# Row maxima of a differential attention branch: 96 rows for each map, or 32 rows with the two maps of a head in two row groups of TensorE

## The chip, the cores and the metric

The kernel runs on one core of one Trainium2 chip. The metric is the device time of one execution in microseconds (us). Lower is better. All times of before are in this document's section on the profile.

## The reference, cut to what matters

The kernel is one layer: a normalized input goes through one input projection, three attention branches (latent attention, differential attention, attention to 256 memory tokens), a gate and an output projection. The differential branch has 4 heads of two softmax maps each, over 2048 tokens, causal:

```python
def diff_branch(dq, dk, dv, pos, qn_g, kn_g, lam_vecs, subln_g, lam_init):
    ...
    q = rope(q, pos).reshape(b, s, DIFF_HEADS, 2, DIFF_D)
    k = rope(k, pos).reshape(b, s, DIFF_HEADS, 2, DIFF_D)
    ...
        sc = jnp.einsum('bqhmd,bkhmd->bhmqk', qblk, k).astype(jnp.float32) * scale
        sc = jnp.where(causal_mask(start, s)[None, None, None], sc, NEG_INF)
        p = jax.nn.softmax(sc, axis=-1)
        a = (p[:, :, 0] - lam * p[:, :, 1]).astype(v.dtype)
    ...
```

`DIFF_D` is 32. The softmax needs a row maximum, or a number near it, before its exponentials. The kernel gets that number in a pass of its own.

## The kernel before, in words

**Numbers as pairs.** Queries, keys, values and weights are kept as two fp16 parts, a high one and a low one. A product of two such numbers is three products: high by high, low by high, high by low. In the differential branch the three stand above each other in one contraction: for each map a column of `kT` (keys) and of `qB` (queries) holds 128 rows, which are 32 rows high, 32 low or high, 32 high or low, and 32 of which the first carries the row maximum (L441 to L461). A matmul over rows 0 to 96 then gives the score with its maximum taken off.

**The row-maximum pass** is `est_block` (L374 to L407). It is called for a step (a group `g` of two heads and a block `b` of 512 queries) and a head `i`, with `nmap` 2 for the differential branch (L464 to L472) and 1 for the latent one. Before, it goes over the maps `m`, then over the four tiles `t` of 128 queries, then over the key blocks `c` up to `b`. For each it multiplies 128 queries by up to 512 keys on rows 0 to 95 (L384), adds the mask on the diagonal with an identity of 128 rows (L386), and reduces the result: for block 0 with a maximum on VectorE (L388), for the others with a copy to bf16 on ScalarE (L390, L393), a maximum of two tiles on VectorE (L394) and a fold at the end of every second `t` (L397 to L399). The tile `er` of that fold has one buffer. The products lie in three PSUM buffers (`pe`). When a head is done, its stack with the maximum is transposed into `qB` (L470), and only then may the scores of that head start.

**What sets the order.** The code is one loop that advances generators (preparation of steps, fills such as projections, heads and tails of softmax maps) by planned positions. Priorities follow from that, and a scheduler then puts the instructions of each engine in an order, so one generator's matmuls stand between those of others. From 200 us to 747 us TensorE does the row-maximum pass and the scores and values of the differential branch (L384, L386, L546, L549, L502 to L505) with projections (L176 to L178) between them. From 747 us to 1340 us the latent branch follows (L812 to L894, its own L384), and to the end the output projection (L930 to L932).

**Other places the change touches.** The memory tokens' keys `mk1` and `mk2` lie in the pool of constants (L200, L201); they are the operands of L632, L653 and L654. The pool `kvp` has five buffers under the tag `kT`, in turn for weights at the start, the memory branch's queries `qA` and the keys `kT` of the differential branch.

Of the kernel before, what the change touches and what calls it, by code (L numbers as in the profile page):

```python
# [19 lines left out]
P = 128  # L20
# [20 lines left out]
def hybrid_block(ctx: ExitStack, tc: tile.TileContext, x, mem, positions, norm_g, w_in, mla_q_norm_g,  # L41
# [21 lines left out]

# [1 line left out]
    ident = cst.tile([P, P], BF16, name="ident")  # L65
# [37 lines left out]

# [1 line left out]
    def stage(name, pool=None):  # L105
# [10 lines left out]
    def load(dst, src, pace=PACE):  # L116
        """At the start, loads take turns with the transposes on the DMA queues."""
        if 0 < len(turned) < 2 * NPACE:
            with tc.issue_after(turned[max(0, len(turned) - pace)].ins):
                SP.dma_start(dst, src)  # L120
        else:
            SP.dma_start(dst, src)
# [18 lines left out]

# [1 line left out]
    def load_w(w, cols, gains, name, out, pool=None, ahead=2, pace=PACE):  # L143
        """Column ranges of w as fp16 pairs: NK views [P, 2, n] appended to out."""
        n = sum(c for _, c in cols)
        kpu = 2 if n > 256 else 4

        def fetch(i):
            st = stage(f"wst_{name}{i}", pool).rearrange("p (k c) -> p k c", k=2)
            at = 0  # L150
            for c0, c in cols:
                load(st[:, :, at:at + c], w[0, 2 * i * P:(2 * i + 2) * P, c0:c0 + c].rearrange("(k p) c -> p k c", p=P), pace)
                at += c
            return st

        sts = [fetch(i) for i in range(ahead - 1)]
        yield 1.0
        for i in range(NK // 2):
            if i + ahead - 1 < NK // 2:
                sts.append(fetch(i + ahead - 1))  # L160
                yield 1.0
            st = sts[i]
            if 2 * i % kpu == 0:
                wt = bigt([P, kpu, 2, 1024 // kpu], f"w_{name}{i}")
            for k in range(2):
                g = gains[:, 2 * i + k:2 * i + k + 1]
                dst = wt[:, (2 * i + k) % kpu]
                A.activation(dst[:, 0, :n], st[:, k, :n], AF.Copy, scale=g)
                V.scalar_tensor_tensor(dst[:, 1, :n], st[:, k, :n], g, dst[:, 0, :n], ALU.mult, ALU.subtract)
                out.append(dst)  # L170
            yield 1.0
# [8 lines left out]
    def project_block(hts, units, n, dst):  # L180
        """dst: [P, 4, >= n]"""
        for t in range(4):
# [10 lines left out]

# [1 line left out]
    top = tc.cur_priority  # L195
# [3 lines left out]
    V.tensor_tensor(g_mk, g_mk, g_mq, ALU.mult)  # L199
    mk1 = cst.tile([P, 2, 4, P], F16, name="mk1")  # L200
    mk2 = cst.tile([P, 2, 4, P], F16, name="mk2")  # L201
    mv = cst.tile([P, 2, 4, 130], F16, name="mv")
# [3 lines left out]
    def mem_kv():  # L206
# [30 lines left out]
        G.memset(s2[:, :, 64:128], MS)  # L237
        SP.dma_start_transpose(mk1.rearrange("p t h k -> p (t h) k"), s1.rearrange("p a b c -> p (a b c)"))
        SP.dma_start_transpose(mk2.rearrange("p t h k -> p (t h) k"), s2.rearrange("p a c -> p (a c)"))
        vv = kv[:, 0:2, 256:512].rearrange("p t (h d) -> p t h d", d=64)  # L240
# [5 lines left out]

# [1 line left out]
    cos_t = cst.tile([P, NT, 16], F32, name="cos_t")  # L248
# [63 lines left out]
    def rope_tabs(b, g, name):  # L312
        """cos and sin of block b's tokens with the halves of the gain folded in."""
        tb = wk.tile([P, 2, 4, 32], F32, tag="rtab", name=f"rt_{name}", bufs=1)
# [9 lines left out]
    def rope(dst, src, tb, nh, eng, name):  # L324
        """dst, src: [P, 4, nh, 32]"""
        tmp = tmp4(f"rtmp_{name}")[:, 0:128 * nh].rearrange("p (t h d) -> p t h d", t=4, d=32)
# [8 lines left out]
    def rope_in_place(q, tb, nh, eng, tmp):  # L335
        """q: [P, 4, nh, 32]"""
        tmp = tmp.rearrange("p (t h d) -> p t h d", t=4, d=32)
# [7 lines left out]

# [1 line left out]
    zsc = dr.tile([3, P, NT, 2 * P], F32, name="zsc")  # L347
# [5 lines left out]
    def put_v(vt, ps):  # L353
        """vt: [P, 2, 130], ps: [P, 2, 64] in PSUM, WS times the values"""
        A.activation(vt[:, :, 0:64], ps, AF.Copy, scale=1.0 / WS)
        V.scalar_tensor_tensor(vt[:, :, 65:129], ps, 1.0 / WS, vt[:, :, 0:64], ALU.mult, ALU.subtract)

    def put_gate(z, ps):
        """2 WS silu of the products ps"""
        A.activation(z, ps, AF.Tanh, scale=0.5 / WS)  # L360
# [10 lines left out]

# [1 line left out]
    def est_block(st, i, nmap, mcol, lhs, rhs):  # L373
        b = st.b  # L374
        mx = sm.tile([P, nmap, 4, 2], F32, tag="mx", name=f"mx{i}_{st.name}", bufs=2)
        fold = b >= EB
        for m in range(nmap):
            for t in range(4):
                if fold and t % 2 == 0:
                    er = wk.tile([P, 2, 512], BF16, tag="er", name="er", bufs=1)  # L380
                for c in range(b + 1):
                    ps = ps_e.tile([P, 512], F32, tag="pe", name="pe")
                    n = (4 if c < b else t + 1) * P
                    T.matmul(ps[:, 0:n], lhsT=lhs(m, t), rhs=rhs(m, c, n // P), start=True, stop=c < b)  # L384
                    if c == b:
# [3 lines left out]
                    elif c == 0:  # L389
                        A.activation(er[:, t % 2], ps, AF.Copy)  # L390
                    else:
                        ec = wk.tile([P, 512], BF16, tag="ec", name="ec", bufs=3)
                        A.activation(ec[:, 0:n], ps[:, 0:n], AF.Copy)  # L393
                        V.tensor_tensor(er[:, t % 2, 0:n], er[:, t % 2, 0:n], ec[:, 0:n], ALU.max)  # L394
                    yield 0.5
                if fold and t % 2:
                    for n in (256, 128, 64):  # L397
# [10 lines left out]

# [1 line left out]
    def prep_d(st, units):  # L410
# [29 lines left out]
        for w in (1, 0):  # L440
# [4 lines left out]
            for i in range(2):  # L445
                dst = stack([P, 4, 2, 4, 32], f"s{w}{i}_{nm}")
                src = r4[:, :, 2 * i:2 * i + 2, :]
                G.memset(dst[:, :, :, 3, :], MS if w else 0.0)
                at_hi, at_lo = ((0, 2), 1) if w else ((0, 1), 2)
                for k in at_hi:  # L450
                    A.activation(dst[:, :, :, k, :], src, AF.Copy)
                V.tensor_tensor(dst[:, :, :, at_lo, :], src, dst[:, :, :, 0, :], ALU.subtract)
                if w:
# [12 lines left out]
        for i in range(2):  # L466
            q4 = st.qs[i].rearrange("p t m r d -> p t m (r d)")
            yield from est_block(st, i, 2, lambda m: q4[:, :, m, 96], lambda m, t: st.qB[i][0:96, t, m, :],
                                 lambda m, c, n: st.kTs[c][0:96, i, 0:n, m, :])
            SP.dma_start_transpose(st.qB[i].rearrange("p t m k -> p (t m) k"), st.qs[i].rearrange("p t m r d -> p (t m r d)"))  # L470
# [3 lines left out]
    class Map:  # L474
        """One softmax map of one block of queries."""

# [39 lines left out]
    def finish(st, y, ct, ys, keep=False):  # L516
        """y: [P, 4, 128], already gated; its fp16 parts go out transposed."""
        b = st.b
# [63 lines left out]

# [1 line left out]
    def prep_m(st, units):  # L584
# [36 lines left out]
    def est_m(st):  # L621
# [6 lines left out]
        for i in range(2):  # L628
            for t in range(4):
                ps = ps_e.tile([P, 512], F32, tag="pe", name="pe")  # L630
                for k in range(2):
                    T.matmul(ps[:, 256 * k:256 * k + 256], lhsT=st.qA[:, i, t, k, :], rhs=mk1[:, :, 2 * i + k, :],  # L632
                             start=(k == 0), stop=(k == 1), skip_group_check=True)
# [8 lines left out]
    def maps_m(st):  # L642
# [7 lines left out]
        for h in range(4):  # L650

            def scores(ps, j, t0, n, diag, h=h):
                T.matmul(ps, lhsT=mk1[:, j, h, :], rhs=st.qA[:, h // 2, :, h % 2, :], start=True, stop=False)  # L653
                T.matmul(ps, lhsT=mk2[:, j, h, :], rhs=st.qB[h // 2][:, :, h % 2, :], start=False, stop=True)  # L654

# [15 lines left out]

# [1 line left out]
    def gates(b, chunk, units):  # L673
        """2 WS silu(z) of two groups for one block, kept in DRAM."""
        for t in range(4):
# [7 lines left out]

# [1 line left out]
    krot, ss_kr = [], []  # L685
# [68 lines left out]

# [1 line left out]
    wuq, wukv = [], []  # L756
# [146 lines left out]

# [1 line left out]
    wout = {}  # L905
# [17 lines left out]
    def out_tile(yt, t, hf, acc):  # L923
        """Adds the product of the given channel tiles to one [128, 512] tile of acc."""
        ps = ps_p.tile([P, 512], F32, tag="pp", name="pp")
# [9 lines left out]
    def out_dm():  # L935
        """x plus the products of the differential and memory channels, kept in DRAM."""
        yield from load_wout(range(4, 8))
# [31 lines left out]
    def out_last():  # L969
        """All but the last channel tile for the last block, kept on chip."""  # L970
        b = NB - 1
# [31 lines left out]

# [1 line left out]
    zcol = 1440  # L1005
# [230 lines left out]
```

## Time and profile before

| what | value |
|---|---|
| median of 3 runs | 1418.45 us |
| lowest and highest run | 1413.12 us, 1423.48 us |
| span of the profiled execution, first to last instruction | 1420.8 us |
| matmuls on TensorE in it | 13552, busy 92% of the span |
| granted TensorE clock, mean | 0.982 of full speed |

The profiled execution has no time of its own beside its span: 1420.8 us lies between the runs, 2.4 us above their median. In the profile, PE is TensorE's matmuls and PEld its weight loads, DVE is VectorE, ACT ScalarE, POOL GpSimd and SP SyncE, which issues the DMAs. A duration of a matmul runs to the modelled end of its pipeline; the next one starts earlier, so the pace is read from the starts.

### The profile page before, as it was taken

The numbers are of one execution on the slowest core, as the hardware profiler recorded it, in microseconds if no ns is written. First come the engines' busy times: TensorE is split into PE (matmuls) and PEld (weight loads), VectorE is DVE, ScalarE is ACT, GpSimd is POOL, SyncE is SP. The second block draws the span as 40 slices with busy tenths as digits, with TensorE's granted clock in tenths as the row PEclk, the third lists the DMA queues.
The fourth block names the chain that finished last, engine by engine and source line by source line (L and its number), as shares of the span: only waits on it lengthen the run. The fifth ranks groups of instructions, "written<-read, shape, count | busy, mean of one in ns | idle before, by whom it ended". The sixth has DMA issues, their size and how long they took to land. (4 is left out here: it accounts for less than half of the span.)

```text
span 1420.8 us, 35214 instructions
## 1 busy us (share of the span) xinstructions
PE 1312.4 (92%) x13552; PEld 831.7 (59%) x13552; DVE 1120.2 (79%) x2649; ACT 897.6 (63%) x2153; POOL 359.8 (25%) x541
## 2 busy tenths in 40 slices
PE   4789899999999999998998999999999899989998
PEld 1344456667676666677775665655655565555554
DVE  3458787889789958888899788977788999975645
ACT  5646444677777747786776676655776788664521
POOL 2222133303052044122321233533124433200000
PEclk9899999999999999999999999999999999999999
DMA  8999754223223223347245156255544454264352
GB/s 211 244 211 196 162 111 100 53 66 69 52 53 76 39 35 64 68 123 196 97 98 134 50 153 167 57 127 125 110 87 87 105 94 75 54 142 153 113 204 78
DMA packets 302696, 157.67 MB, mean 111 GB/s; under 512 B 248384, under 2 KB 281280, under 8 KB 302528
## 3 DMA queue, kind: packets, MB, share of 16 engines
q1 hardware_dynamic: 302496, 155.42, 47.6%
q8 instruction: 106, 1.74, 0.5%
q14 instruction: 62, 0.51, 0.1%
q0 software_dynamic: 32, 0.00, 0.0%
HBM read 61.79 MB, written 34.34 MB: 68 GB/s over the span
## 5 line engine op out<-in xcount | busy, mean ns | idle before, releaser
L492 ACT ACTIVATE p<-st 128x512 f32<-128x512 f32 (+3 forms) x672 | 354.6, 547 | 177.6 <-PE st L892 60.5
L493 DVE TENSOR_TENSOR plo<-p 128x512 f16<-128x512 f32 (+3 forms) x672 | 407.5, 617 | 60.1 <-ACT p L492 56.0
L505 PEld LDWEIGHTS <-plo 128*128 128x128 f16 x2304 | 217.5, 99 | 52.1 <-DVE plo L493 31.8
L502 PEld LDWEIGHTS <-p 128*128 128x128 bf16 x2304 | 219.1, 98 | 49.0 <-issue 2.3
L504 PEld LDWEIGHTS <-p 128*128 128x128 bf16 x2304 | 218.2, 98 | 29.4 <-issue 0.6
L393 ACT ACTIVATE ec<-pe 128x512 bf16<-128x512 f32 (+3 forms) x384 | 196.3, 537 | 40.5 <-PE pe L386 18.8
L394 DVE TENSOR_TENSOR er<-er,ec 128x512 bf16<-128x512 bf16 (+3 forms) x384 | 143.6, 380 | 33.5 <-ACT ec L393 20.4
L502 PE MATMUL pv<-V_d,p 128*128 128x65 f16 x1088 | 140.8, 193 | 0.8 <-DVE y_d L557 0.8
L504 PE MATMUL pv<-V_d,p 128*128 128x64 f16 x1088 | 140.7, 195 | 0.0
L502 PE MATMUL pv<-V_a,p 128*128 128x65 f16 x1088 | 139.4, 194 | 0.2
L504 PE MATMUL pv<-V_a,p 128*128 128x64 f16 x1088 | 139.2, 195 | 0.0
L505 PE MATMUL pv<-V_d,plo 128*128 128x65 f16 x1088 | 134.8, 192 | 4.5 <-DVE plo L493 3.9
L505 PE MATMUL pv<-V_a,plo 128*128 128x65 f16 x1088 | 130.6, 193 | 8.5 <-DVE plo L493 7.9
L390 ACT ACTIVATE er<-pe 128x512 bf16<-128x512 f32 x192 | 109.6, 604 | 38.3 <-DVE mx_d L399 14.2
L176 PEld LDWEIGHTS <-ht_x 128*128 128x128 f16 x896 | 88.5, 99 | 70.9 <-DMA ht_x<-xh_x 20.2
L890 PE MATMUL st<-qB_a,kT_a 97*128 97x512 f16 (+1 forms) x320 | 112.1, 350 | 18.0 <-ACT p L492 17.2
L177 PEld LDWEIGHTS <-ht_x 128*128 128x128 f16 x896 | 88.4, 99 | 55.5 <-issue 9.3
L178 PEld LDWEIGHTS <-ht_x 128*128 128x128 f16 x896 | 88.4, 99 | 54.5 <-DMA ht_x<-xl_x 4.6
L546 PE MATMUL st<-qB_d,kT_d 97*128 97x512 f16 (+1 forms) x320 | 109.2, 349 | 9.1 <-ACT p L492 8.3
L384 PE MATMUL pe<-kT_d,qB_d 96*128 96x512 f16 (+2 forms) x320 | 106.0, 350 | 8.2 <-ACT ec L393 4.7
L891 PE MATMUL st<-qB_a,kT_a 96*128 96x512 f16 (+1 forms) x320 | 112.0, 350 | 0.0
L892 PE MATMUL st<-qB_a,kT_a 96*128 96x512 f16 (+1 forms) x320 | 111.4, 348 | 0.0
(285 smaller groups left out, 3383.9 us busy)
## 6 DMA issues: line engine op xcount, KB each, us to landing
xt_x<-in_x_dram SPq DMA_DIRECT2D x16, 512.0 KB, 4.6
xr<-in_x_dram SPq DMA_DIRECT2D x16, 512.0 KB, 3.6
part<-xr SPq DMA_DIRECT2D x16, 512.0 KB, 3.0
ysc<-yt SPq DMA_DIRECT2D x31, 256.0 KB, 2.2
yl<-ysc SPq DMA_DIRECT2D x15, 512.0 KB, 4.3
zsc<-zc SPq DMA_DIRECT2D x48, 128.0 KB, 2.3
xa<-part SPq DMA_DIRECT2D x12, 512.0 KB, 3.6
out_dram<-xa SPq DMA_DIRECT2D x12, 512.0 KB, 2.7
```

What stands on the lines that cost most here:

```text
L390: A.activation(er[:, t % 2], ps, AF.Copy)
L393: A.activation(ec[:, 0:n], ps[:, 0:n], AF.Copy)
L394: V.tensor_tensor(er[:, t % 2, 0:n], er[:, t % 2, 0:n], ec[:, 0:n], ALU.max)
L492: A.activation(p32[:, :n], ps[:, :n], AF.Exp, scale=self.scale)
L493: V.tensor_tensor(plo[:, :n], p32[:, :n], phi[:, :n], ALU.subtract)
L502: T.matmul(pvv[:, t, 0:65], lhsT=phi[:, c], rhs=vt[:, 0:65], start=(j == 0 and t == 0), stop=False, skip_group_check=True)
L504: T.matmul(pvv[:, t, 0:64], lhsT=phi[:, c], rhs=vt[:, 65:129], start=False, stop=False, skip_group_check=True)
L505: last["pv"] = T.matmul(pvv[:, t, 0:65], lhsT=plo[:, c], rhs=vt[:, 0:65], start=False, stop=(j == self.njt - 1), skip_group_check=True)
L546: T.matmul(ps[:, :n], lhsT=st.kTs[j // 4][0:97, h, j % 4, m % 2, :], rhs=st.qB[h][0:97, t0:4, m % 2, :], start=True, stop=not diag)
L890: T.matmul(ps[:, :n], lhsT=kt[0:97, h, j % 4, 0, :], rhs=q[0:97, 0, t0:4, :], start=True, stop=False)
L891: T.matmul(ps[:, :n], lhsT=kt[0:96, h, j % 4, 0, :], rhs=q[0:96, 1, t0:4, :], start=False, stop=False)
L892: T.matmul(ps[:, :n], lhsT=kt[0:96, h, j % 4, 1, :], rhs=q[0:96, 0, t0:4, :], start=False, stop=not diag)
```

## The change

The pass goes over `t`, then `c`, and inside that over both maps. The matmul of map `m` reads rows 32m to 32m + 31 only, which hold the high parts of both operands (so the row maximum comes from the high parts alone). For this the second map's stack has its parts in another order: rows 32 to 63 of its keys and queries are now high parts. The mask still takes an identity of 128 rows. `er` gets two buffers, for both branches. To make room, `mk1` and `mk2` become one tile in the pool `kvp` under the tag `kT`.

```diff
-    mk1 = cst.tile([P, 2, 4, P], F16, name="mk1")
-    mk2 = cst.tile([P, 2, 4, P], F16, name="mk2")
+    mk = []
...
+        mk12 = kvp.tile([P, 2, 2, 4, P], F16, tag="kT", name="mk12")
+        mk.extend([mk12[:, 0], mk12[:, 1]])
...
     def est_block(st, i, nmap, mcol, lhs, rhs):
...
-        for m in range(nmap):
-            for t in range(4):
-                if fold and t % 2 == 0:
-                    er = wk.tile([P, 2, 512], BF16, tag="er", name="er", bufs=1)
-                for c in range(b + 1):
-                    ps = ps_e.tile([P, 512], F32, tag="pe", name="pe")
-                    n = (4 if c < b else t + 1) * P
-                    T.matmul(ps[:, 0:n], lhsT=lhs(m, t), rhs=rhs(m, c, n // P), start=True, stop=c < b)
+        ers = {}
+        for t in range(4):
+            if fold and t % 2 == 0:
+                for m in range(nmap):
+                    ers[m] = wk.tile([P, 2, 512], BF16, tag="er", name=f"er{m}", bufs=2)
+            for c in range(b + 1):
+                n = (4 if c < b else t + 1) * P
+                pss = [ps_e.tile([P, 512], F32, tag="pe", name="pe") for m in range(nmap)]
+                for m in range(nmap):
+                    T.matmul(pss[m][:, 0:n], lhsT=lhs(m, t), rhs=rhs(m, c, n // P), start=True, stop=c < b)
+                for m in range(nmap):
+                    ps = pss[m]
                     if c == b:
                         T.matmul(ps[:, t * P:n], lhsT=ident, rhs=mask_e, start=False, stop=True)
...
-                at_hi, at_lo = ((0, 2), 1) if w else ((0, 1), 2)
+                rows = dst.rearrange("p t m r d -> p t (m r) d")
+                at_hi, at_lo = ((slice(0, 5, 4), slice(2, 6, 3)), slice(1, 7, 5)) if w else \
+                    ((slice(0, 6, 5), slice(1, 7, 5)), slice(2, 5, 2))
                 for k in at_hi:
-                    A.activation(dst[:, :, :, k, :], src, AF.Copy)
-                V.tensor_tensor(dst[:, :, :, at_lo, :], src, dst[:, :, :, 0, :], ALU.subtract)
+                    A.activation(rows[:, :, k, :], src, AF.Copy)
+                V.tensor_tensor(rows[:, :, at_lo, :], src, rows[:, :, at_hi[0], :], ALU.subtract)
...
-            yield from est_block(st, i, 2, lambda m: q4[:, :, m, 96], lambda m, t: st.qB[i][0:96, t, m, :],
-                                 lambda m, c, n: st.kTs[c][0:96, i, 0:n, m, :])
+            yield from est_block(st, i, 2, lambda m: q4[:, :, m, 96], lambda m, t: st.qB[i][32 * m:32 * m + 32, t, m, :],
+                                 lambda m, c, n: st.kTs[c][32 * m:32 * m + 32, i, 0:n, m, :])
```

The order of the instructions moves with it. In the kernel after, the matmul of the pass is L387 and its mask L391. On TensorE, at the start of the pass for block 3 of the first group, head 0 (`qB0_d03`), before; `pe` with its number is the PSUM tile of one product, `kT_d00` the keys of block 0:

```order
L384 LDWEIGHTS qB0_d03_4536
L384 MATMUL pe_4614<-kT_d00_1900,qB0_d03_4536 128x512
L384 LDWEIGHTS qB0_d03_4536
L384 MATMUL pe_4637<-kT_d01_2407,qB0_d03_4536 128x512
L176 LDWEIGHTS ht_x1_191
L176 MATMUL pp_5897<-w_d12_5684,ht_x1_191 128x512
```

The same place now:

```order
L515 MATMUL pv_4445<-V_d01_2120,plo_4567 128x65
L387 LDWEIGHTS qB0_d03_4535
L387 MATMUL pe_4614<-kT_d00_1899,qB0_d03_4535 128x512
L387 LDWEIGHTS qB0_d03_4535
L387 MATMUL pe_4615<-kT_d00_1899,qB0_d03_4535 128x512
L387 LDWEIGHTS qB0_d03_4535
L387 MATMUL pe_4640<-kT_d01_2406,qB0_d03_4535 128x512
L178 LDWEIGHTS ht_x15_955
L178 MATMUL pp_5974<-w_z00_1812,ht_x15_955 128x256
```

Here `pe_4614` and `pe_4615` are the two maps of one product, next to each other, and the first map of the next key block follows. In the whole order 16 of the 160 pairs stand like that, and 16 more times a second map's matmul is followed at once by the next first map's.

On TensorE in the pass for block 2 (`qB0_d02`), before, one matmul of the pass between projections:

```order
L178 MATMUL pp_4020<-w_z02_2154,ht_x6_495 128x256
L384 LDWEIGHTS qB0_d02_3287
L384 MATMUL pe_3311<-kT_d01_2407,qB0_d02_3287 128x512
L177 LDWEIGHTS ht_x13_831
L177 MATMUL pp_3972<-w_d03_1464,ht_x13_831 128x512
```

In the same pass now, one pair:

```order
L177 MATMUL pp_4410<-w_z00_1812,ht_x8_599 128x256
L387 LDWEIGHTS qB0_d02_3286
L387 MATMUL pe_3509<-kT_d00_1899,qB0_d02_3286 128x512
L178 LDWEIGHTS ht_x8_599
L178 MATMUL pp_4410<-w_z00_1812,ht_x8_599 128x256
L556 LDWEIGHTS kT_d00_1899
L556 MATMUL st_4001<-qB1_d01_2457,kT_d00_1899 128x512
L176 LDWEIGHTS ht_x8_599
L176 MATMUL pp_4410<-w_z00_1812,ht_x8_599 128x256
L387 LDWEIGHTS qB0_d02_3286
L387 MATMUL pe_3510<-kT_d00_1899,qB0_d02_3286 128x512
L177 LDWEIGHTS ht_x8_599
```

`pe_3509` and `pe_3510` are the two maps of one product; two projection matmuls and one score matmul, of 97 to 128 rows each, stand between them. In 144 of the 160 pairs something stands between, most often 1 to 19 matmuls. The 320 matmuls of the pass form 288 runs of matmuls on 32 rows, each between matmuls on 97 to 128 rows.

## Rows read from the trace of the kernel before

**Rows 1.** The page: span, busy time of each engine, granted TensorE clock.
```profile
span 1420.8 us, 35214 instructions
...
PE 1312.4 (92%) x13552; PEld 831.7 (59%) x13552; DVE 1120.2 (79%) x2649; ACT 897.6 (63%) x2153; POOL 359.8 (25%) x541
...
PEclk9899999999999999999999999999999999999999
```

**Rows 2.** Busy time of each engine by stage (window, its length, then the columns named).
```profile
core 0: us, PE busy (x) PEld busy (x) DVE busy (x) ACT busy (x) POOL busy (x), PEclk, DMA share, GB/s
...
200.00:747.00 547.00, 527.57 (x5870) 369.95 (x5869) 457.62 (x1194) 381.33 (x989) 146.64 (x183) 0.99 0.36 81
747.00:1340.00 593.00, 546.50 (x6081) 344.30 (x6079) 497.74 (x1164) 392.59 (x944) 163.24 (x254) 0.98 0.46 107
```

**Rows 3.** Timeline of TensorE: start us, duration us, line, operands.
```profile
560.71 0.33 PE L384 MATMUL pe<-kT_d,qB_d 96*128 96x384 f16 x1
560.88 0.22 PE L386 MATMUL pe<-mask_e,ident 128*128 128x128 bf16 x1
560.93 0.27 PE L176 MATMUL pp<-w_lq,ht_x 128*128 128x256 f16 x1
561.04 0.27 PE L177 MATMUL pp<-w_lq,ht_x 128*128 128x256 f16 x1
561.15 0.38 PE L384 MATMUL pe<-kT_d,qB_d 96*128 96x512 f16 x1
561.37 0.27 PE L178 MATMUL pp<-w_lq,ht_x 128*128 128x256 f16 x1
...
568.27 0.19 PE L505 MATMUL pv<-V_d,plo 128*128 128x65 f16 x1
568.30 0.20 PE L502 MATMUL pv<-V_d,p 128*128 128x65 f16 x1
```

**Rows 4.** Waits of TensorE, 200 to 747 us: total us, times, longest.
```profile
PE st L546 <- ACT p L492: 5.2, 10, 2.0
PE pe L384 <- ACT ec L393: 4.7, 7, 1.6
PE pv L505 <- DVE plo L493: 2.7, 3, 2.0
```

**Rows 5.** Matmuls of the pass by shape, 200 to 747 us: xcount, busy us, mean ns, idle before.
```profile
L384 PE MATMUL pe<-kT_d,qB_d 96*128 96x512 f16 x224 | 82.7, 383 | 5.2 <-ACT ec L393 3.0 <-DMA qB_d<-s_d 1.1 <-ACT er L390 1.0
...
L384 PE MATMUL pe<-kT_d,qB_d 96*128 96x384 f16 x32 | 10.6, 331 | 1.5 <-ACT ec L393 0.7 <-ACT er L390 0.6 <-DVE mx_d L388 0.2
...
L384 PE MATMUL pe<-kT_d,qB_d 96*128 96x256 f16 x32 | 8.7, 273 | 1.0 <-ACT ec L393 1.0
...
L384 PE MATMUL pe<-kT_d,qB_d 96*128 96x128 f16 x32 | 7.0, 220 | 0.4 <-DMA qB_d<-s_d 0.3
```

**Rows 6.** Weight loads of the pass, whole span.
```profile
L384 PEld LDWEIGHTS <-qB_d 96*128 96x128 f16 x320 | 30.7, 98 | 11.4 <-DMA qB_d<-s_d 2.0 <-issue 0.6
```

**Rows 7.** Line L390, whole span: what ScalarE sat idle for (us, times).
```profile
  DVE mx_d L399: 14.2, 15
  DVE mx_a L399: 12.0, 15
```

**Rows 8.** Waits of TensorE, 747 us to the end.
```profile
PE st L890 <- ACT p L492: 17.2, 22, 1.8
```

**Rows 9.** Copies into the stacks, 200 to 747 us.
```profile
L451 ACT ACTIVATE s_d<-qkv_d 128x256 f16<-128x256 f32 x60 | 20.3, 408 | 8.1 <-DVE qkv_d L443 7.9 <-issue 0.2
```

**Rows 10.** Timelines: the memory branch's last score matmul; the second key block's transposes.
```profile
222.44 0.38 PE L654 MATMUL st<-qB_m,mk 128*128 128x512 f16 x1
...
235.73 2.66 SPq L460 DMA_TRANSPOSE kT_d<-s_d  x2
```

More of the change, by code (lines that the diff above doesn't have):

```diff
@@ L237, in mem_kv @@
         G.memset(s2[:, :, 64:128], MS)
-        SP.dma_start_transpose(mk1.rearrange("p t h k -> p (t h) k"), s1.rearrange("p a b c -> p (a b c)"))
-        SP.dma_start_transpose(mk2.rearrange("p t h k -> p (t h) k"), s2.rearrange("p a c -> p (a c)"))
+        mk12 = kvp.tile([P, 2, 2, 4, P], F16, tag="kT", name="mk12")
+        mk.extend([mk12[:, 0], mk12[:, 1]])
+        SP.dma_start_transpose(mk[0].rearrange("p t h k -> p (t h) k"), s1.rearrange("p a b c -> p (a b c)"))
+        SP.dma_start_transpose(mk[1].rearrange("p t h k -> p (t h) k"), s2.rearrange("p a c -> p (a c)"))
         vv = kv[:, 0:2, 256:512].rearrange("p t (h d) -> p t h d", d=64)
@@ L389, in est_block @@
                     elif c == 0:
-                        A.activation(er[:, t % 2], ps, AF.Copy)
+                        A.activation(ers[m][:, t % 2], ps, AF.Copy)
                     else:
+                        er = ers[m]
                         ec = wk.tile([P, 512], BF16, tag="ec", name="ec", bufs=3)
@@ L394, in est_block @@
                         V.tensor_tensor(er[:, t % 2, 0:n], er[:, t % 2, 0:n], ec[:, 0:n], ALU.max)
-                    yield 0.5
-                if fold and t % 2:
+                yield 0.5 * nmap
+            if fold and t % 2:
+                for m in range(nmap):
+                    er = ers[m]
                     for n in (256, 128, 64):
@@ L631, in est_m @@
                 for k in range(2):
-                    T.matmul(ps[:, 256 * k:256 * k + 256], lhsT=st.qA[:, i, t, k, :], rhs=mk1[:, :, 2 * i + k, :],
+                    T.matmul(ps[:, 256 * k:256 * k + 256], lhsT=st.qA[:, i, t, k, :], rhs=mk[0][:, :, 2 * i + k, :],
                              start=(k == 0), stop=(k == 1), skip_group_check=True)
@@ L652, in scores @@
             def scores(ps, j, t0, n, diag, h=h):
-                T.matmul(ps, lhsT=mk1[:, j, h, :], rhs=st.qA[:, h // 2, :, h % 2, :], start=True, stop=False)
-                T.matmul(ps, lhsT=mk2[:, j, h, :], rhs=st.qB[h // 2][:, :, h % 2, :], start=False, stop=True)
+                T.matmul(ps, lhsT=mk[0][:, j, h, :], rhs=st.qA[:, h // 2, :, h % 2, :], start=True, stop=False)
+                T.matmul(ps, lhsT=mk[1][:, j, h, :], rhs=st.qB[h // 2][:, :, h % 2, :], start=False, stop=True)
             def done(o, rl, h=h):
```

## Prediction

> **What bounds the kernel now.** I read the page first: TensorE is busy for 1312.4 of 1420.8 us, and its granted clock stands near full speed throughout [rows 1], so the question is whether its queue sets the pace where the change works. The table by stage answers: from 200 to 747 us, the whole of the differential branch's pass, TensorE is busy 527.57 of 547 us, while VectorE is busy 457.62 and ScalarE 381.33 [rows 2]. That leaves 19.4 us idle. Because busy time counts modelled ends, I then read starts in the timeline: matmuls follow each other at 0.22 us for 512 columns, 0.17 for 384, 0.11 for 256, 0.05 for 128 and 0.03 for 65, with nothing between them [rows 3]. The stream of columns is the limit there. Its waits are few: the three largest total 12.6 us [rows 4]. What is added to or taken from TensorE's queue in this stage reaches the end nearly in full. From 747 to 1340 us the same engine has 46.5 us idle [rows 2], and its largest wait is for ScalarE's exponentials, 17.2 us [rows 8].
>
> **The matmuls of the pass.** There are 224 of 512 columns and 32 each of 384, 256 and 128 [rows 5]. At the paces of [rows 3] they hold the stream for 224 x 0.22 + 32 x (0.17 + 0.11 + 0.05) = 59.8 us. Fewer rows do not shorten one of them: a matmul on 96 rows goes at the same pace per column as one on 128 [rows 3]. Only two maps running at once would, and all 160 pairs would save half, 29.9 us.
>
> **How many can.** The order decides. The two maps of a product are neighbours in 16 of 160 pairs; with the 16 places where a second map is followed by the next first map there are 32 neighbours in different row groups. The shorter of the two has 512 columns in 20 of them, 384 in 4, 256 in 3 and 128 in 5. Full overlap saves 20 x 0.22 + 4 x 0.17 + 3 x 0.11 + 5 x 0.05 = 5.7 us; no overlap saves 0. I take 4, since starts are never quite together. For the other pairs something that uses all rows stands between, and nothing overlaps.
>
> **What the small matmuls may cost.** Before, every matmul uses 96 rows or more, and going from 96 to 128 and back costs no time: the 384-column matmul at 560.71 us is followed after 0.17 us by a 128-row one [rows 3]. After, the queue has 288 runs on 32 rows between matmuls on nearly all rows, 576 edges. No row of before has such an edge, so I bound it. Below, an edge is as free as that one: 0. Above, each edge waits until the matmul ahead has left the array, and its weight load is no longer hidden. A matmul's tail after its last column is its duration less its pace, 0.38 - 0.22 = 0.16 us, and for 65 columns 0.19 - 0.03, the same [rows 3]. A weight load takes 98 ns [rows 6]. So 288 x 2 x (0.16 + 0.10) = 150 us above. I take one tail for each run, 288 x 0.16 = 46 us: a result that passes one row group comes out sooner than one that passes four, so at least the entry should wait for what is in flight, while the other edge need not. That it waits at all is my assumption; the tail is the nearest measured length for it.
>
> The Trainium skill, TensorEngine Tiling (Array Packing), Key Properties, speaks for a wait: changing the tiling mode, not just the tile, drains the engine. It gives no time. By it both edges would wait, the second rival below; without it the first one holds. Nothing in the trace of before can show it.
>
> **What absorbs it.** A slower TensorE lets its waits for ScalarE and VectorE shrink. The 19.4 us idle in this stage is the most that could vanish; I take 6, about half of the 12.6 us in the three waits of [rows 4].
>
> **The second buffer of `er`.** ScalarE sits idle before L390 for 12.0 us in the latent branch and 14.2 us in the differential one, until the last fold of the tile before has been read [rows 7]. With two buffers the wait of the latent branch goes, as there is one map. In the differential branch two maps now take two buffers, so a pair again waits for the folds of the pair before: nothing changes. ScalarE is not the bound, so of the 12.0 us only what TensorE feels counts, through its 17.2 us of waiting for exponentials [rows 8]. Late after that are the many other waits on the exponentials' path. Between 0 and 12 I take 3.
>
> **Costs of nothing.** The copies into the stacks keep their number and their 256 elements a partition, 408 ns each [rows 9]; only strides differ, and ScalarE has 165 us idle in the stage, which hides up to some tens of ns more for each. The folds, copies and maxima of the pass keep number and size. `mk12` takes a turn in the `kT` buffers: the second key block of the differential branch takes its buffer. Its transposes are issued at 235.73 us, the memory branch's last score starts at 222.44 [rows 10], so 13 us hide that wait. If that cover were gone, the two transposes, the other issues behind them on SP and that block's pass would be late by the lack. No DMA is added.
>
> **Sum**, against the profiled span: 46 - 4 - 6 - 3 = +33 us, 1420.8 + 33 = 1453.8. The span lies 2.4 us above the median of the runs, so the forecast for the median is 1451 us, 2.3% slower.
>
> **Rivals.**
> 1. *The edges are free, and so are few of the pairs: the change doesn't do what it says.* 4 + 3 us saved: 1418.45 - 7 = 1411 us, 0.5% faster, not to be told from no change (about 1%, 14.2 us, is what a measurement of this kernel can tell). For it: rows may change between 96, 97 and 128 at no cost. Against: those all use all four row groups. Own range 1404 to 1418.
> 2. *Both edges wait for a tail.* 2 x 46 = 92 us, of which the stage's idle absorbs 12, less 4 and 3: +73, so 1491 us. With every weight load exposed as well it is 150 - 19 = +131 before the small gains, near 1543. For it: TensorE's stream has no slack to hide an edge [rows 2, 3]. Against: the prefetch of weights ahead of running matmuls, whose loads cost nothing before, may go on.
> 3. *Faster, by the buffer of `er`.* If ScalarE's stalls before L390 in the latent branch stand in the way of the exponentials directly, all 12.0 us return, and the neighbours overlap in full, with free edges: 12.0 + 5.7 = 17.7 us, 1401 us. It decides from about 8.5 us of the 12.0 on, where the total passes 14.2. For it: TensorE's largest wait there is on ScalarE [rows 8]. Against: ScalarE is busy 392.59 of 593 us [rows 2], and it would have to be the last to arrive each time.
>
> The Trainium skill, TensorE: Matmul & The Clock Gate, Part 3 (The mechanism), has matmuls in different row groups start about 4 ns apart. By that the neighbours would give all of the 5.7 us instead of 4, an estimate from its rule at this trace's paces; no run shows it yet.
>
> **How the numbers follow.** Forecast 0.40, its own range 1430 to 1475; rival 1 0.32; rival 2 0.18; rival 3 0.10. Slower by over 1% takes the forecast but 0.02 of it, and rival 2: 0.56. Faster by over 1% takes rival 3 and 0.02 of rival 1: 0.12. Within 1%: 0.32. The range that holds 8 in 10 reaches from 1406, which leaves out rival 3 and the low edge of rival 1 (0.12), to 1500, which leaves out 0.08 of rival 2.
>
> **What would show it.** In the changed trace, the starts around L387: if a 128-row matmul before it or behind it keeps the pace of [rows 3], the edge is free and rival 1 holds; a gap of about 0.16 us on one side is the forecast, on both sides rival 2. Neighbouring L387 should start much closer than 0.22 us. The stage from 200 to 747 us should grow by some 35 us, and the latent branch shrink by about 3, with the wait of L395 for the fold gone there. I am wrong if L387's neighbours show gaps and the stage doesn't grow, or if the latent branch moves by more than 12 us.

## The result, and the profile after

The kernel after takes 1484.53 us (median of 4 runs, 1483.17 to 1486.61), the one before beside it 1417.3 us. The ratio is 1.0469, 95% interval 1.0443 to 1.0495: 67 us slower. The forecast was 1451 us; 1484.5 lies above the forecast's own range (1430 to 1475) and inside the wider one that was to hold in 8 cases of 10 (1406 to 1500).

The page's first lines and its row of the clock, to be read against [rows 1]:

```profile
span 1482.9 us, 35262 instructions
...
PE 1369.0 (92%) x13552; PEld 828.4 (56%) x13552; DVE 1117.4 (75%) x2649; ACT 904.2 (61%) x2153; POOL 360.9 (24%) x541
...
PEclk9999999999999999999999999999999998999999
```

The same number of matmuls, and TensorE is busy 57 us longer (1369.0 against 1312.4). The other engines are busy for what they were, ScalarE 7 us more (904.2 against 897.6). Next, the table by stage, cut where each kernel's branches end: from the memory branch's last score to the differential branch's last, and from there to the latent branch's last. Columns are those of [rows 2]. First the kernel before:

```profile
222.00:813.00 591.00, 565.24 (x6500) 395.25 (x6498) 496.78 (x1281) 417.99 (x1072) 155.40 (x200) 0.99 0.36 81
813.00:1402.00 589.00, 548.25 (x5849) 340.04 (x5846) 470.05 (x1080) 365.65 (x871) 151.64 (x230) 0.98 0.47 113
```

The kernel after:

```profile
223.00:859.00 636.00, 616.61 (x6504) 391.64 (x6503) 495.99 (x1280) 422.69 (x1069) 159.52 (x200) 0.98 0.34 75
859.00:1464.00 605.00, 552.39 (x5833) 340.73 (x5830) 467.10 (x1079) 365.85 (x871) 148.27 (x230) 0.97 0.46 110
```

Two stages lost time, not one. The differential stage is 45 us longer, with TensorE busy 51 us more. The latent stage, whose matmuls the change does not touch, is 16 us longer, and there TensorE is busy only 4 us more: it waits. Its granted clock is lower there as well, 0.97 against 0.98.

The timeline of TensorE in the kernel after (start us, duration us, line), one lone matmul of the pass, then three neighbours printed as one row:

```profile
400.13 0.23 PE L178 MATMUL pp<-w_lk,ht_x 128*128 128x160 f16 x1
400.20 0.23 PE L176 MATMUL pp<-w_lk,ht_x 128*128 128x160 f16 x1
400.37 0.39 PE L387 MATMUL pe<-kT_d,qB_d 32*128 32x512 f16 x1
400.69 0.24 PE L177 MATMUL pp<-w_lk,ht_x 128*128 128x160 f16 x1
400.77 0.19 PE L515 MATMUL pv<-V_d,plo 128*128 128x65 f16 x1
...
373.74 0.60 PE L387 MATMUL pe<-kT_d,qB_d 32*128 32x512 f16 x3
```

A projection matmul of 160 columns is followed after 0.07 us by the next (400.13 to 400.20). Before the 32-row one the same step takes 0.17 us, and the 32-row one of 512 columns is followed after 0.32 us, where [rows 3] has 0.22. So each edge costs 0.10 us, on both sides. Over all edges at which the profile names no wait, I took start to start less the columns ahead at 2.4 GHz, the upper of the clock's two levels: the medians are 98 ns on the way in (281 edges) and 104 ns on the way out (286), against 3 and 6 ns in the kernel before. They add up to 58 us, where the same places add up to 5 us in the kernel before.

The neighbours do overlap. Three matmuls of 512 columns take 0.60 us from the first start to the last end: the first two start together, and the third, which needs the first one's row group, 0.22 us later. Of the 32 neighbours 22 start within 0.01 us of each other; their starts save 3.9 us. Six of the other ten stand like that third one, behind a pair that still holds their row group.

Waits of TensorE in the latent stage of the kernel after (total us, times, longest), and what ScalarE sat idle for before L395, the former L390 of [rows 7], over the whole span:

```profile
PE st L900 <- ACT p L502: 25.7, 26, 2.6
```

```profile
  PE pe L387: 20.4, 30
  DVE mx_d L407: 3.4, 3
```

The wait for the fold in the latent branch (`mx_a`, 12.0 us) is gone, as the second buffer would have it, and that in the differential branch fell from 14.2 us to 3.4. Yet TensorE's wait for exponentials in the latent stage rose from 17.2 us [rows 8] to 25.7.

### The profile page after: what moved, and what is told of

The parts are those of the page before. It is cut to its first block, busy times and chain, and to the rows that moved or that the text cites. A ratio compares the mean times of both kernels' runs of the same rounds, so it can differ in the third digit from the quotient of the medians.

```text
span 1482.9 us, 35262 instructions
## 1 busy us (share of the span) xinstructions
PE 1369.0 (92%) x13552; PEld 828.4 (56%) x13552; DVE 1117.4 (75%) x2649; ACT 904.2 (61%) x2153; POOL 360.9 (24%) x541
## 4 chain that ended last, share of the span: by engine, by line
PE 63%; DMA 11%; DVE 10%; POOL 6%; ACT 5%; issue 3%; SPq 2%; ACTq 0%; DVEq 0%; POOLq 0%
PE pe L387 7%; PE pp L177 7%; PE pp L178 7%; PE pp L176 7%; PE pv L515 4%; PE pv L514 4%; PE pv L512 3%; PE st L556 3%; DMA qB_a<-qs_a 3%; PE pp L940 3%; PE pp L941 3%; PE pp L942 3%; DVE plo L503 3%; DMA kT_a<-ks_a 2%; PE st L900 2%
## 5 line engine op out<-in xcount | busy, mean ns | idle before, releaser
L399 ACT ACTIVATE ec<-pe 128x512 bf16<-128x512 f32 (+3 forms) x384 | 200.2, 540 | 60.3 <-PE pe L387 28.2
L900 PE MATMUL st<-qB_a,kT_a 97*128 97x512 f16 (+1 forms) x320 | 113.2, 354 | 26.4 <-ACT p L502 25.7
L395 ACT ACTIVATE er<-pe 128x512 bf16<-128x512 f32 x192 | 116.0, 612 | 24.6 <-PE pe L387 20.4
L387 PE MATMUL pe<-kT_d,qB_d 32*128 32x512 f16 (+3 forms) x320 | 104.7, 354 | 3.3 <-DMA qB_d<-s_d 1.8
```

Of the source, the lines that this page charges most:

```text
L387: T.matmul(pss[m][:, 0:n], lhsT=lhs(m, t), rhs=rhs(m, c, n // P), start=True, stop=c < b)
```

## The experiments

**96 rows again, all else as after.**

```diff
-    lambda m, t: st.qB[i][32 * m:32 * m + 32, t, m, :],
-    lambda m, c, n: st.kTs[c][32 * m:32 * m + 32, i, 0:n, m, :])
+    lambda m, t: st.qB[i][0:96, t, m, :],
+    lambda m, c, n: st.kTs[c][0:96, i, 0:n, m, :])
```

> The kernel after, with both maps of the pass on rows 0 to 95 again; everything else (maps in turn, second er buffer, mk12 in the kvp pool, order of the parts) stays. Theory A, the time is lost at the 576 edges between 32-row and full-row matmuls: they are gone, 1405 to 1420 us. Theory B, the time is lost by the new order of the pass (maps in turn, both waiting for PSUM and folds): it stays at 1475 to 1490 us.

Measured: 1444.2 us, ratio 1.0198 (1.0174 to 1.0222). Between both theories. The 32 rows cost 40 us here (1484.5 less 1444.2), and something else in the change costs 27. Its timeline has a matmul of the pass between its neighbours at the old pace, 0.22 us:

```profile
373.79 0.38 PE L387 MATMUL pe<-kT_d,qB_d 96*128 96x512 f16 x1
374.01 0.38 PE L178 MATMUL pp<-w_d,ht_x 128*128 128x512 f16 x1
```

**32 rows alone, in the kernel before.**

```diff
-    lambda m, t: st.qB[i][0:96, t, m, :],
-    lambda m, c, n: st.kTs[c][0:96, i, 0:n, m, :])
+    lambda m, t: st.qB[i][0:32, t, m, :],
+    lambda m, c, n: st.kTs[c][0:32, i, 0:n, m, :])
```

> The kernel before, with the pass on rows 0 to 31 for both maps (high parts alone, one row group, nothing can overlap), its order otherwise kept; its order has 304 runs of such matmuls. Theory A: 304 runs at 0.10 us for each of two edges, 61 us on TensorE, 1472 to 1485 us. Theory B: the order is that of before, 1412 to 1424 us.

Measured: 1459.94 us, ratio 1.0321 (1.0284 to 1.0358). The edges are as long as they were (medians 98 and 104 ns, 62 us in sum), as two starts show:

```profile
300.50 0.38 PE L178 MATMUL pp<-w_d,ht_x 128*128 128x512 f16 x1
300.81 0.38 PE L384 MATMUL pe<-kT_d,qB_d 32*128 32x512 f16 x1
301.13 0.39 PE L176 MATMUL pp<-w_d,ht_x 128*128 128x512 f16 x1
```

Steps of 0.31 and 0.32 us, where 512 columns took 0.22. But the 62 us, 57 more than the same places hold in the kernel before, came out as 44 at the end. The stage from 224 to 856 us is 41 us longer than the 591 of before, and TensorE's other waits in it (start to start less columns, where TensorE sat idle before a start) shrank from 39 to 21 us: that is the absorption, 18 us and not the 6 that I had taken. Theory A is right on the edges and too high on what reaches the end.

**The second buffer and the new place of the memory keys alone, in the kernel before.**

```diff
-    er = wk.tile([P, 2, 512], BF16, tag="er", name="er", bufs=1)
+    er = wk.tile([P, 2, 512], BF16, tag="er", name="er", bufs=2)
...
+    mk12 = kvp.tile([P, 2, 2, 4, P], F16, tag="kT", name="mk12")
```

> The kernel before with the second er buffer and mk12 in the kvp pool alone; maps one after the other, 96 rows. Theory A: no edges; the second buffer gives back 0 to 6 us, 1411 to 1419 us. If the loss came from mk12's place in the pool (theory C), 1450 us or more.

Measured: 1428.18 us, ratio 1.0075 (1.005 to 1.01), neither of the two. The differential stage kept its length (220 to 813 us); the latent one took 594 us. So the second buffer, or the pool, costs time in the stage where I had counted a gain.

**All pairs neighbours.**

```diff
+    if nmap == 2:
+        for m in range(2):
+            tc.cur_priority -= 2000 * m
+            d = T.matmul(pss[m][:, 0:8], lhsT=ident, rhs=mask_e[:, 0:8], start=True, stop=True)
+            tc.cur_priority += 2000 * m
+        tc.cur_priority -= 2000
+        with tc.issue_after(d.ins):
+            for m in range(2):
+                T.matmul(pss[m][:, 0:n], lhsT=lhs(m, t), rhs=rhs(m, c, n // P), start=True, stop=c < b)
+        tc.cur_priority += 2000
...
```

The lines with `cur_priority` ask the scheduler to keep the pair together.

> The kernel after with the two matmuls of every pair next to each other on TensorE: ahead of them stand two matmuls of 8 columns on all rows into the same two PSUM buffers (they are overwritten and only hold the pair back until both buffers are free). 160 runs instead of 288, 160 neighbours instead of 32. Theory A: edges 160 x 0.2 = 32 us, overlap 30 us back, the small matmuls about 320 x 0.03 = 10 us: 12 us over a version without edges, 1420 to 1436 us. If the cost hung on each small matmul and not on the edges of a run (theory D), 320 x 0.18 - 30 + 10 = 38 us over it, 1448 to 1460 us.

Measured: 1457.07 us, ratio 1.0281 (1.0234 to 1.0328). That is above theory A's range and inside theory D's (1448 to 1460), but both ranges stood on a version without edges at some 1408 to 1424 us, and the one that was measured, the first experiment, took 1444.2. Against that it is 13 us, near theory A's 12 and not D's 38. The timeline bears on the two theories more directly:

```profile
601.88 0.27 PE L176 MATMUL pp<-w_lq,ht_x 128*128 128x256 f16 x1
601.99 0.17 PE L389 MATMUL pe<-mask_e,ident 128*128 128x8 bf16 x1
602.09 0.39 PE L394 MATMUL pe<-kT_d,qB_d 32*128 32x512 f16 x2
602.41 0.28 PE L177 MATMUL pp<-w_lq,ht_x 128*128 128x256 f16 x1
```

Two matmuls of 512 columns are done with in 0.32 us from their start to the next one's: 0.22 for both, and 0.10 for the edge. All 160 pairs overlap, which saves 28.5 us, and the 320 edges cost 34, both counted from the starts as above. At one pair a run, overlap does not quite pay for the edges. The agreement of 13 with 12 is in part chance, as the stages show, first in the version with 96 rows, then with all pairs neighbours:

```profile
221.00:820.00 599.00, 572.01 (x6508) 399.06 (x6506) 491.99 (x1282) 418.04 (x1071) 165.59 (x200) 0.97 0.35 79
820.00:1423.00 603.00, 554.61 (x5846) 341.90 (x5843) 467.83 (x1080) 365.31 (x872) 149.07 (x230) 0.97 0.46 111
...
221.00:840.00 619.00, 587.96 (x6806) 400.17 (x6805) 495.37 (x1289) 417.28 (x1068) 146.88 (x201) 0.96 0.34 76
840.00:1433.00 593.00, 547.03 (x5847) 338.23 (x5844) 469.25 (x1079) 365.10 (x871) 147.36 (x230) 0.99 0.45 113
```

The differential stage is 20 us longer, and the latent stage, which the edit does not touch, 10 shorter. Of the 20, some 7 are longer waits and 7 are columns that took longer at 1.2 GHz, the lower of the clock's two levels, at which TensorE stood for 51 us of this stage against 31; edges and small matmuls less overlap are the rest.

**One buffer for the latent branch, in the kernel after.**

```diff
-    ers[m] = wk.tile([P, 2, 512], BF16, tag="er", name=f"er{m}", bufs=2)
+    ers[m] = wk.tile([P, 2, 512], BF16, tag=f"er_{nmap}", name=f"er{m}", bufs=nmap)
```

> The kernel after, with one er buffer for the latent branch (as before) and two for the differential one. Theory L, the second er buffer costs time in the latent stage, where it lets the copies of the pass run ahead of the exponentials on ScalarE: the latent stage, 605 us from the last differential score to the last latent one, falls to about 590, and the whole to 1466 to 1474 us. Theory M, the latent stage lost its time to the shift of the whole order, not to the buffer: 1480 to 1488 us.

Measured: 1464.16 us, ratio 1.0325 (1.0298 to 1.0351), 2 us below theory L's range and far from theory M's. The buffer costs 20 us. The latent stage fell to 583 us:

```profile
861.00:1444.00 583.00, 545.06 (x5836) 337.70 (x5834) 469.57 (x1080) 365.05 (x871) 151.13 (x230) 0.99 0.47 114
```

Of the 22 us by which it fell, TensorE's waits (counted as in the second experiment) make up 14. The other 8 are columns at the lower clock: in the kernel after, TensorE stood at 1.2 GHz for 34 us of this stage, here for 14. Each of the seven falls of the clock in that stage of the kernel after came shortly after an idle time of 1.3 to 2.9 us on TensorE. These parts are from one profiled execution of each kernel; over all four executions of each, the mean granted clock keeps the same order (0.968 to 0.976 against 0.976 to 0.981).

**The same with 96 rows** (the edits of the first experiment and of this one).

```diff
-    lambda m, t: st.qB[i][32 * m:32 * m + 32, t, m, :],
+    lambda m, t: st.qB[i][0:96, t, m, :],
...
+    ers[m] = wk.tile([P, 2, 512], BF16, tag=f"er_{nmap}", name=f"er{m}", bufs=nmap)
```

> The first experiment (96 rows, maps in turn) with one er buffer for the latent branch. Theory L: latent stage from 603 to about 590 us, the whole 1426 to 1434 us. Theory M: 1440 to 1448 us.

Measured: 1429.82 us, ratio 1.0083 (1.0055 to 1.0111). Theory L again. With one latent buffer, the price of 32 rows is 1464.2 - 1429.8 = 34 us; here the latent buffer makes 14 us of difference (1444.2 - 1429.8).

**The second buffer for the latent branch alone, in the kernel before** (with `mk12` in the pool; the differential branch keeps one buffer).

```diff
-    er = wk.tile([P, 2, 512], BF16, tag="er", name="er", bufs=1)
+    er = wk.tile([P, 2, 512], BF16, tag=f"er_{nmap}", name="er", bufs=3 - nmap)
```

> The kernel before with mk12 in the kvp pool and a second er buffer for the latent branch alone (the differential branch keeps one, and TensorE's runs of the pass are those of before). Theory L: latent stage 6 to 14 us longer than 589, the whole 1423 to 1432 us. Theory M: 1413 to 1421 us.

Measured: 1427.9 us, ratio 1.0066 (1.0042 to 1.0091), as theory L has it.

**`mk12` in the pool alone, in the kernel before.**

```diff
-    mk1 = cst.tile([P, 2, 4, P], F16, name="mk1")
-    mk2 = cst.tile([P, 2, 4, P], F16, name="mk2")
...
+    mk12 = kvp.tile([P, 2, 2, 4, P], F16, tag="kT", name="mk12")
```

> The kernel before with mk12 in the kvp pool alone, er with one buffer. Theories L and M both: no change, 1412 to 1421 us. If the pool's slot costs time (theory C): 1425 us or more.

Measured: 1418.49 us, ratio 1.0006 (0.999 to 1.0022). The pool's slot costs nothing, so the last two differ by the buffer alone, and it costs 9 us here. Their latent stages, with one buffer and with two:

```profile
814.00:1398.00 584.00, 546.32 (x5839) 338.65 (x5836) 470.25 (x1080) 365.32 (x871) 150.80 (x230) 0.99 0.48 114
...
813.00:1407.00 594.00, 550.06 (x5847) 340.50 (x5846) 467.73 (x1079) 365.43 (x871) 147.40 (x230) 0.97 0.46 112
```

Half of the 10 us are waits of TensorE and half are columns at the lower clock (31 us at 1.2 GHz against 17). ScalarE's waits in the latent stage (total us, times, longest), with one buffer:

```profile
ACT p L493 <- PE pv L506: 19.3, 23, 3.5
ACT er L391 <- DVE mx_a L400: 12.6, 15, 1.7
...
ACT qs_a L861 <- DMA kT_a<-ks_a: 8.3, 7, 2.1
```

and with two:

```profile
ACT p L493 <- PE pv L506: 37.1, 33, 7.0
ACT qs_a L861 <- DMA kT_a<-ks_a: 19.4, 9, 5.1
```

The 12.6 us for the fold are gone, and the waits for values (L506) and for a key transpose (`kT_a`) grew by 29 us together. My reading is that the freed copies come earlier on ScalarE, so that the exponentials and the next head's copies stand where what they need is later. That the waits moved is shown; why they grew is argued from these rows only.

**32 rows for one head of two** (with one latent buffer).

```diff
+    lambda m, t: st.qB[i][slice(32 * m, 32 * m + 32) if i == 0 else slice(0, 96), t, m, :],
+    lambda m, c, n: st.kTs[c][slice(32 * m, 32 * m + 32) if i == 0 else slice(0, 96), i, 0:n, m, :])
```

> The kernel after with one er buffer for the latent branch, and the 32-row matmuls for the first head of each step alone; the second head's pass reads rows 0 to 95 again. 134 runs on 32 rows instead of 288. Theory A: the 34 us between 1430 us (all on 96 rows) and 1464 us (all on 32 rows) go by the number of runs, 34 x 134 / 288 = 16 us over 1430: 1441 to 1451 us. If the loss came once 32-row matmuls are used at all, or from something else that both heads share: 1460 us or more, or 1430.

Measured: 1441.9 us, ratio 1.0163 (1.0127 to 1.0198): 12 us over the version without edges, with 134 of 288 runs, where the rule of three gives 16. The loss goes with the number of runs, within what the intervals (0.35%, 5 us) allow.

**64 rows** (with one latent buffer).

```diff
+    lambda m, t: st.qB[i][0:64, t, m, :],
+    lambda m, c, n: st.kTs[c][0:64, i, 0:n, m, :])
```

> The kernel after with one er buffer for the latent branch and both maps of the pass on rows 0 to 63, the lower half of the array (parts high by high and low by high or high by low). Theory A, if any number of rows that leaves row groups out has edges: 0.10 us on each side and no overlap of neighbours, 1464 to 1474 us. If only 32-row matmuls have them: 1426 to 1434 us.

Measured: 1470.41 us, ratio 1.0372 (1.0329 to 1.0415). Half of the array has the same edges:

```profile
400.58 0.23 PE L176 MATMUL pp<-w_lk,ht_x 128*128 128x160 f16 x1
400.75 0.39 PE L387 MATMUL pe<-kT_d,qB_d 64*128 64x512 f16 x1
401.07 0.24 PE L177 MATMUL pp<-w_lk,ht_x 128*128 128x160 f16 x1
```

0.17 and 0.32 us, as with 32 rows. The median on the way in is 98 ns, on the way out 106, and neighbours no longer overlap (each follows the one ahead at the pace of its columns and 13 ns more).

**One PSUM buffer at a time** (96 rows, maps in turn, one latent buffer).

```diff
-    pss = [ps_e.tile([P, 512], F32, tag="pe", name="pe") for m in range(nmap)]
...
+    for m in range(nmap):
+        ps = ps_e.tile([P, 512], F32, tag="pe", name="pe")
+        T.matmul(ps[:, 0:n], lhsT=lhs(m, t), rhs=rhs(m, c, n // P), start=True, stop=c < b)
```

> The kernel of 96 rows, maps in turn and one latent er buffer (1430 us), but a map's PSUM buffer is taken only when its own matmul comes and its mask, copy and maximum follow before the other map's matmul. Theory P, the 11 us between that kernel and the one with the maps one after the other (1418.5 us) come from taking two of the three PSUM buffers at once: 1415 to 1422 us. Theory O, they come from the order of the loop (both maps' folds fall together, and both wait for the pair of er buffers): 1426 to 1433 us.

Measured: 1431.68 us, ratio 1.0107 (1.0068 to 1.0146). Theory P falls: the 11 us of the maps in turn do not come from two PSUM buffers taken at once. What is left between the two versions is the order of the loop, its coarser step (it now gives way to the other generators once for a pair, by a `yield` that the diff above does not show), the pair of `er` buffers of the differential branch and the new order of the parts in the stacks. No run tells these apart. Of the 11 us, 7 to 8 lie in the differential stage, with `mk12` moved and then with 96 rows and maps in turn:

```profile
222.00:814.00 592.00, 566.07 (x6505) 396.22 (x6504) 497.21 (x1281) 417.64 (x1071) 155.86 (x200) 0.99 0.35 80
...
221.00:820.00 599.00, 570.08 (x6479) 397.20 (x6476) 490.67 (x1279) 416.46 (x1068) 164.16 (x200) 0.98 0.35 79
```

By the starts, 4 of them are longer waits of TensorE and 4 columns at the lower clock (27 us at 1.2 GHz against 14).

No version beat the kernel before.

## Why the prediction was right in direction and short in size

The versions stand in a row: before with `mk12` moved 1418.5 us; maps in turn on 96 rows with one latent buffer and all that belongs to the new order 1429.8 (+11); the same on 32 rows 1464.2 (+34); with the second latent buffer, which is the kernel after, 1484.5 (+20). With the buffer put in ahead of the 32 rows, the row reads +11, +14 and +40. Two terms of the prediction failed: the second buffer of `er`, with its sign, and the order of the loop, which was put at nothing. The edges were right in mechanism but too small. Against its steps:

- **TensorE's queue sets the pace from 200 to 747 us.** Right in kind, as time added to TensorE's queue there is later at the end; but "nearly in full" was too much. About seven to eight tenths come through: 44 us of 57 with 32 rows in the old order (1459.9 less 1416.1), 34 of 49 (58 of edges, less the 5 of before and 4 of overlap) in the new one. The term "what absorbs it" was taken as 6 us; TensorE's waits in the stage shrank by 18 us in the old order and by 14 in the new one (from 43 with 96 rows to 29 with 32, both with one latent buffer).
- **How many can overlap.** Right in size, 4 us taken and 3.9 by the starts, and the pairs that something separates gained nothing. The reason given was not right: neighbours that overlap do start together, within 0.01 us, and half of what lacks of the 5.7 us lies in six runs of three, whose third matmul has to wait for its row group. The sum had counted all 32 as free to overlap.
- **What the small matmuls may cost.** The mechanism was right and the count of edges half of it. I took one tail of 0.16 us a run, 46 us, on the argument that a result that passes one row group comes out sooner, so that the way out need not wait. It does, and nothing here shows the sooner result: the profile gives the pass's matmuls of 512 columns 387 ns on 32 rows and 383 on 96 [rows 5], by ends that are modelled. Both edges cost 0.10 us, 58 us in all. The second rival had both edges, at 0.16 us each, and so 92 us. Its 1491 us is nearest to the result by a sum whose parts are not those measured. The rule of the Trainium skill that I set beside it (TensorEngine Tiling (Array Packing), Key Properties: a change of tiling mode drains the engine) agrees with the trace in that TensorE waits on both sides, and for 64 rows as for 32; each such change cost 0.10 us here. That is less than the tail of 0.16 us, so whether the engine empties in that time these runs do not show.
- **The second buffer of `er`.** This step failed, with its sign. I bounded it between 0 and 12 us of gain, as if a wait that goes could only help, and it cost 20 us in the kernel after, 14 with 96 rows and 9 in the old order. The wait for the fold went, ScalarE's waits for values and key transposes grew by more, TensorE waited longer for the exponentials, and its clock was lower for longer. The fold's wait in the differential branch, which I had said would stay, fell from 14.2 us to 3.4; no gain from that can be seen, as the differential stage with the second buffer alone kept its length.
- **Costs of nothing.** `mk12` costs nothing, as said. The stacks' copies too: L451's 408 ns became 414. The new order of the pass costs 11 us, which I had not priced: I counted that the folds keep their number and size, and not that they move. Which part of the new order it is stays open; 4 of these us are waits of TensorE in the differential stage and 4 its lower clock there.

So +33 us was 46 - 4 - 6 - 3, and +66 is 34 (58 - 5 - 4 = 49, less some 15 absorbed) + 20 + 11. The first part, 34, is near the 36 that the forecast had for edges, overlap and absorption (46 - 4 - 6), but by luck: the edges and the absorption were both taken too small, and the two errors nearly cancel. The other half of the loss comes from what the forecast had as a gain of 3 us and as nothing. The latent branch moved by more than the 12 us that I had named as what would make me wrong there, and it did so the other way.

## What to carry to other kernels

Read the order of the engine before counting on concurrent row groups: pairs that a scheduler separates gain nothing, and each run of matmuls on part of the rows between full ones pays 0.10 us at each end here, together about what one overlapped pair of 512 columns gives back. Put many part-row matmuls into one run, or leave them on the full array, where rows cost nothing. And price a second buffer from both sides: it removes a wait, but moves the instructions that the wait had held. Where the waits of TensorE grow, read its granted clock in the same window, as a part of the loss can lie there.

## What was not expected of the hardware

The way out of a part-row matmul costs as much as the way in (104 and 98 ns), and 64 rows as much as 32. A run's weight load did not get longer for it: those of the pass average 91 ns on 32 rows against 98 [rows 6], but they start late:

```profile
L387 PEld LDWEIGHTS <-qB_d 32*128 32x128 f16 x320 | 26.5, 91 | 47.0 <-issue 32.1 <-DMA qB_d<-s_d 2.8 <-PE pe L387 0.3
```

Their engine sat idle for 47.0 us before them, 11.4 before [rows 6]. With 96 rows in the new order (the first experiment) it is 14.3, so most of this comes with the 32 rows.
